# A decoder block on one Trainium2 core: the sums of one kept weight pair are tied, on VectorE, behind the last copies of a block inverse

## The chip, the cores and the metric

The kernel runs on one core of a Trainium2 chip. The metric is the device time of one execution in microseconds (us), less being better; a run's number is the median of its timed executions. The engines are called as in the profile: PE (TensorE, matrix products; PEld is its weight loads), DVE (VectorE), ACT (ScalarE), POOL (GpSimd) and SP (SyncE, which here only issues transfers). Each engine works through its own queue of instructions in order.

## The reference, cut to what matters

One transformer block on 256 tokens of width 2048, all in float32. A projection feeds two branches: a gated delta rule (heads of 128, solved in triangular blocks) and a sparse attention over the 64 best keys. Both are gated, merged, projected and normalised, and a gated feed-forward layer with a hidden width of 5632 follows.

```python
a = m + jnp.eye(CHUNK, dtype=f32)
u = lax.linalg.triangular_solve(a, v_beta, left_side=True, lower=True, unit_diagonal=True)
...
merged = jax.nn.sigmoid(gate_a) * (o_a @ w_branch_a[l]) + jax.nn.sigmoid(gate_b) * (o_b @ w_branch_b[l])
x = layer_norm(DEEPNORM_ALPHA * x + merged @ w_out[l], ln1_g[l], ln1_b[l])
h_gate, h_up = jnp.split(x @ w_ffn_in[l], 2, axis=-1)
x = layer_norm(DEEPNORM_ALPHA * x + (jax.nn.silu(h_gate) * h_up) @ w_ffn_out[l], ln2_g[l], ln2_b[l])
```

Two places of this computation meet in the change: the triangular solve (as an explicit inverse of each block) and the feed-forward weights of `w_ffn_in`.

## The kernel before, in words

**The stream of weights.** Nearly all of the time goes into products of the 256 tokens with weights that are streamed from memory. A weight chunk of 128 x 1024 goes through `chunk` (L84 to L94): SP issues its load into `raw` (L89), ACT rounds it to `hi` (L91), DVE takes the rest `lo = raw - hi` (L93), and PE multiplies with both parts. There are four buffers each of `raw`, `hi` and `lo`: SP's load waits until DVE has taken the `lo` of the chunk four places earlier, and ACT's cast waits until PE has finished that earlier chunk. In the stretch that the change touches, `group_ws` (L140) runs four chunks to a group; one chunk is sixteen matmuls of L153 and sixteen of L156, and a group's result is joined on ACT and DVE (L163, L164).

**Small work between the chunks.** After each chunk `tick` lets the waiting chains (generators) emit their next step, so that the work of the delta rule and of the attention stands between the chunks of the projection. Its products use four PSUM tiles called `aux`, the streams four called `acc`.

**Who sets the order.** PE's and SP's instructions stand as the code emits them. Those of DVE, ACT and POOL are put in order by a scheduler, from the data that they read and write and from a priority: `tc.high_priority(offset=LEAD)` moves a step forward, a negative offset moves it back.

**The block inverse.** `key_chain` inverts the triangular blocks: 32 x 32 blocks by substitution, then `merge(32)` and `merge(64)` (L589) join neighbouring blocks. A merge has three steps. L606 multiplies, two `aux` tiles, copied into `s_ak` by ACT (L612) and by DVE (L610). L617 transposes sixteen tiles in four groups of four, one `aux` tile a group; groups 0 and 2 are copied into `s_t` by ACT (L623), groups 1 and 3 by DVE (L621). L631 multiplies `s_t` with `s_ak`, and DVE puts the result into `s_u` (L638 in `merge(32)`, L636 in `merge(64)`). The `aux` tile of L617's last group is one that ACT's copy of group 0 (L623) sets free.

**The kept pairs.** The feed-forward products take pairs of weight rows with seven products in place of eight, for which sums of the weights are needed. For five groups (`KEPT`) the sums of the first pair are made early: `kept_chain` (L941) loads a pair into a raw buffer (L950, two transfers on SP), `four_sums` (L930) makes four sums on DVE (L934, L935, L938, L939), these are cast on ACT (L960) and their rests taken on DVE (L961), and POOL stores both (L963, L964) to memory (`d_s`), from where the feed-forward stage loads them from 851 us on. The chain takes pairs 0 to 3 one after another; pairs 0 and 2 use one raw buffer (`k_rawoh_`), pairs 1 and 3 another (`k_raws_x`), and all share one buffer for the casts (`k_hiol_`). So pair 2's load waits for pair 0's stores. All its DVE and ACT steps have a negative priority offset.

**What follows.** `late_form` writes `f_room` (L1059) into the buffer of pairs 1 and 3, so its first DVE instruction waits for the stores of pair 3; `z_chain` loads `z_wraw` into the buffer of pairs 0 and 2.

Of the kernel before, what the change touches and what calls it, by code (L numbers as in the profile page):

```python
# [8 lines left out]
F32 = mybir.dt.float32  # L9
# [3 lines left out]
OP = mybir.AluOpType  # L13
# [4 lines left out]
P = 128  # L18
# [14 lines left out]
LEAD = 70  # L33
# [30 lines left out]
def block_kernel(ctx: ExitStack, tc: tile.TileContext, xT, x, cpack, onehot, relb, convw, alog, dtb, gnw,  # L64
                 ws, wws, win, wz, wgt, wba, wbb, woa, wob, wfi, wfg, wfo, ln1g, ln1b, ln2g, ln2b, out):
    nc = tc.nc
# [3 lines left out]
    sm = ctx.enter_context(tc.tile_pool(name="sm", bufs=1, side="left"))  # L70
# [4 lines left out]
    def ps_aux():  # L75
        return aux.tile([P, 512], F32, name="aux", tag="aux")
# [42 lines left out]
    def event(name):  # L119
        done[name] = clock[0]  # L120
# [220 lines left out]
    def T(name, shape, dtype=F32, tag=None):  # L341
        return p1.tile(shape, dtype, name=name, tag=tag or name)
# [35 lines left out]
    def t16(name):  # L378
        return T(name, [P, NTB, H])
# [204 lines left out]

    rk2, rk, nb, nbe, rkb = t16("rk2"), t16("rk"), t16("nb"), t16("nbe"), t16("rkb")
    rq2, rq, fo = t16("rq2"), t16("rq"), t16("fo")
    d_m = dr.tile([4, NTB * H, 32, 32], F32, name="d_m")
    d_x = dr.tile([4, NTB * H, 32, 32], F32, name="d_x")

    def merge(b):  # L590

        n = P // (2 * b)
        hi = (64, P) if n == 1 else (0, P)
        w = 64 if n == 1 else 96
        uv = s_u.rearrange("p t (n two b) -> p t n two b", two=2, b=b)
        if n == 1:
            mp, up = mnv[:, :, 0:64], s_u[:, :, 0:64]
        else:
            mp = s_sq.rearrange("p (t c) -> p t c", c=64)
            up = s_e.rearrange("p a h d -> p (a h d)")[:, 0:1024].rearrange("p (t c) -> p t c", c=64)  # L600
            nc.scalar.copy(up.rearrange("p t (n b) -> p t n b", n=n), uv[:, :, :, 0, :])
        for q in range(2):
            a = ps_aux()
            for i in range(8):
                t = q * 8 + i
                nc.tensor.matmul(a[0:64, i * 64:(i + 1) * 64], mp[hi[0]:hi[1], t, :], uv[hi[0]:hi[1], t, :, 1, :],  # L606
                                 start=True, stop=True)
            dst = s_ak[0:64, q * 512:(q + 1) * 512]
            if q % 2:
                nc.vector.tensor_copy(dst, a[0:64])  # L610
            else:
                nc.scalar.copy(dst, a[0:64])  # L612
                yield 1
        for q in range(4):
            a = ps_aux()
            for i in range(4):
                nc.tensor.transpose(a[0:64, i * w:(i + 1) * w], up[0:w, q * 4 + i, :], ident[0:w, 0:w])  # L617
            dst = s_t[0:64, q * 4:q * 4 + 4, 0:w]
            src = a[0:64, 0:4 * w].rearrange("p (t d) -> p t d", t=4)
            if q % 2:  # L620
                nc.vector.tensor_copy(dst, src)  # L621
            else:
                nc.scalar.copy(dst, src)  # L623
            if q == 1:
                yield 1
        yield 2
        for q in range(2):
            a = ps_aux()
            for i in range(8):
                t = q * 8 + i  # L630
                nc.tensor.matmul(a[0:w, i * 64:(i + 1) * 64], s_t[0:64, t, 0:w], s_ak[0:64, t * 64:(t + 1) * 64],  # L631
                                 start=True, stop=True)
            dst = uv[0:w, q * 8:q * 8 + 8, :, 1, :]
            src = a[0:w].rearrange("p (t n b) -> p t n b", t=8, b=b)
            if n == 1:
                nc.vector.tensor_copy(dst, src)  # L636
            else:
                nc.vector.tensor_tensor(dst, src, dst, op=OP.add)  # L638
            yield 1 if q == 0 else 3


    def key_chain():
# [53 lines left out]
        yield INV_WAIT  # L696
        yield "qc1s"
        yield from merge(32)
        yield from merge(64)
        event("inv")  # L700

# [225 lines left out]

    d_s = dr.tile([len(KEPT), 2, P, 2, 1024], F32, name="d_s")

    def four_sums(ra, rb, lead=0):  # L930

        r0, r1, s0, s1 = (t[:, n * 512:n * 512 + 512] for t in (ra, rb) for n in range(2))
        with tc.high_priority(offset=lead):
            nc.vector.tensor_add(r0, r0, s1)  # L934
            nc.vector.tensor_add(s1, r1, s1)  # L935
        yield 1
        with tc.high_priority(offset=lead):
            nc.vector.tensor_add(r1, r0, r1)  # L938
            nc.vector.tensor_add(s0, r1, s0)  # L939

    def kept_chain(ms, wait, old, old_hi, gap, ev):  # L941
        yield wait
        raws = [T(f"k_raw{t}", [P, 2, 1024], tag=t) for t in old]
        hi = T(f"k_hi{old_hi}", [P, 2, 1024], F32R, tag=old_hi)
        for m in ms:
            if gap and m > ms[0]:
                yield gap
            raw = raws[m % len(old)]
            for i in range(2):
                nc.sync.dma_start(raw[:, i], wfg[KEPT[m] - 1, i])  # L950
                yield 1
            yield 1
            for _ in four_sums(raw[:, 0], raw[:, 1], -LEAD):
                yield 1
            yield 1
            for i in range(2):
                with tc.high_priority(offset=-LEAD):
                    for n in range(2):
                        cs = slice(n * 512, n * 512 + 512)
                        nc.scalar.copy(hi[:, i, cs], raw[:, i, cs])  # L960
                        nc.vector.tensor_sub(raw[:, i, cs].bitcast(F32R), raw[:, i, cs], hi[:, i, cs].bitcast(F32))  # L961
                yield 1
                nc.gpsimd.dma_start(d_s[m, 0, :, i], hi[:, i].bitcast(F32))  # L963
                nc.gpsimd.dma_start(d_s[m, 1, :, i], raw[:, i])  # L964
        event(ev)

    start(kept_chain(range(4), KEPT_FROM, ("oh_", "s_x"), "ol_", 0, "kept0"))
    conv_first(s_kT, pss)
    event("kc0")
# [193 lines left out]
    for tag in ("thi", "tlo"):  # L1163
        gates_home[tag][0] = 0
    start(early_chain(wgt[2], (2, 4), ga_ready, "gaready"))
    start(kept_chain(range(4, 5), 1, ("s_x",), "s_rv", 5, "kept1"))
    for j in range(4):
        js = slice(j * 512, (j + 1) * 512)
# [447 lines left out]
    for j in (1, 2, 3):  # L1616
        nc.vector.scalar_tensor_tensor(v1[j], v1[j], mv[:, 0:1], gt2[:, slice(j * 512, j * 512 + 512)],
                                       op0=OP.subtract, op1=OP.mult)
    for j in (1, 2, 3):
        nc.vector.scalar_tensor_tensor(v1[j], v1[j], rs, bt2[:, slice(j * 512, j * 512 + 512)],  # L1620
                                       op0=OP.mult, op1=OP.add)
# [113 lines left out]
```

## Time and profile before

| | us |
|---|---|
| median of 3 runs | 1452.83 |
| these runs | 1451.66, 1452.83, 1455.95 |
| the profiled execution's own time | 1453.58 |
| its span in the profile | 1451.8 |
| PE busy | 1443.1 |
| DVE busy | 1283.2 |
| ACT busy | 816.6 |
| POOL busy | 58.3 |

The span is what the hardware profiler saw from the first instruction to the last; the 1.8 us between it and the execution's own time lie around it. Starts in the timelines count from the start of the span. A row of a timeline gives start, duration, engine, line, operation, tile written and tile read, the count, and in brackets the idle time of the engine ahead of it and what ended that. The granted PE clock was 0.998 of full speed over the span.

### The profile page before, as it was taken

How to read it: one execution, taken by the hardware profiler on the slowest of the kernel's cores; microseconds unless marked ns; L12 is line 12 of the kernel's file. 1: busy time of each engine (PE TensorE's matmuls, PEld its weight loads, DVE VectorE, ACT ScalarE, POOL GpSimd, SP SyncE). 2: the span in 40 equal slices, each digit the busy share in tenths (PEclk: the TensorE clock that was granted, in tenths of full speed). 3: DMA queues.
4: the chain of work that ended last, by engine and by line, in shares of the span. 5: the costliest groups of instructions: out<-in, count | busy, mean ns of one | idle time of the engine just before them, and what ended most of it. 6: DMA issues, size and time to landing. Idle time of an engine off the chain costs nothing.

```text
span 1451.8 us, 19648 instructions
## 1 busy us (share of the span) xinstructions
PE 1443.1 (99%) x7137; PEld 1214.2 (84%) x7137; DVE 1283.2 (88%) x1769; ACT 816.6 (56%) x1025; POOL 58.3 (4%) x79
## 2 busy tenths in 40 slices
PE   9999999999999999999999999999999999999998
PEld 8888888888888888888888888888888888888886
DVE  6798988789799969998897899999999998989987
ACT  5765454557556646655445565656566565554552
POOL 0001011121000000000000000000000000000000
PEclk9999999999999999999999999999999999999999
DMA  8656589854456775766865777677766666888863
GB/s 290 196 162 196 174 213 335 287 188 159 171 202 221 264 248 201 249 186 208 296 210 202 244 263 281 244 267 257 279 214 211 213 218 247 313 338 269 318 210 116
DMA packets 102833, 339.81 MB, mean 234 GB/s; under 512 B 17792, under 2 KB 18984, under 8 KB 102224
## 3 DMA queue, kind: packets, MB, share of 16 engines
q1 hardware_dynamic: 88800, 311.35, 62.1%
q0 software_dynamic: 6752, 24.85, 5.0%
q10 hardware_dynamic: 7184, 2.36, 0.7%
q8 instruction: 56, 0.92, 0.3%
q14 instruction: 41, 0.34, 0.1%
HBM read 314.19 MB, written 24.31 MB: 233 GB/s over the span
## 4 chain that ended last, share of the span: by engine, by line
PE 98%; DMA 1%; ACT 0%; DVE 0%; issue 0%; POOLq 0%; SPq 0%; ACTq 0%; DVEq 0%
PE acc L217 11%; PE acc L218 11%; PE acc L219 11%; PE acc L153 10%; PE aux L217 10%; PE aux L219 10%; PE aux L218 10%; PE acc L156 5%; PE acc L173 4%; PE acc L175 4%; PE acc L174 4%; PE aux L174 2%; PE aux L175 2%; PE aux L173 1%; PE aux L737 1%; DMA k_rawoh__2366<-in_wfg_dram 1%
## 5 line engine op out<-in xcount | busy, mean ns | idle before, releaser
L91 ACT CAST hi<-raw 128x1024 fp32r<-128x1024 f32 (+1 forms) x384 | 392.9, 1033 | 326.7 <-PE acc L219 71.7
L93 DVE TENSOR_TENSOR lo<-raw,hi 128x1024 fp32r<-128x1024 f32 (+1 forms) x384 | 458.9, 1205 | 82.4 <-ACT hi L91 78.4
L153 PE MATMUL acc<-X,hi 128*128 128x512 f32 x640 | 203.7, 400 | 0.0
L217 PE MATMUL acc<-hi,X 128*128 128x512 f32 x370 | 145.2, 392 | 0.0
L219 PE MATMUL acc<-hi,X 128*128 128x512 f32 x370 | 144.1, 389 | 0.0
L218 PE MATMUL acc<-lo,X 128*128 128x512 f32 x370 | 144.0, 389 | 0.0
L156 PEld LDWEIGHTS acc<-X,lo 128*128 128x128 f32 x640 | 120.2, 188 | 28.3
L156 PE MATMUL acc<-X,lo 128*128 128x256 f32 x640 | 126.0, 278 | 0.0
L217 PE MATMUL aux<-hi,X 128*128 128x512 f32 x306 | 119.7, 391 | 0.0
L219 PE MATMUL aux<-hi,X 128*128 128x512 f32 x306 | 119.2, 389 | 0.0
L218 PE MATMUL aux<-lo,X 128*128 128x512 f32 x306 | 119.1, 389 | 0.0
L153 PEld LDWEIGHTS acc<-X,hi 128*128 128x128 f32 x640 | 97.5, 189 | 2.0 <-ACT hi L91 0.7
L241 ACT CAST f_thi<-f_wt 128x1024 fp32r<-128x1024 f32 x60 | 63.2, 1053 | 59.7 <-DVE f_wt L246 23.8
L219 PEld LDWEIGHTS acc<-hi,X 128*128 128x128 f32 x370 | 69.4, 188 | 14.5
L217 PEld LDWEIGHTS acc<-hi,X 128*128 128x128 f32 x370 | 69.5, 188 | 14.3 <-ACT s_u L979 0.4
L218 PEld LDWEIGHTS acc<-lo,X 128*128 128x128 f32 x370 | 69.5, 188 | 14.0
L242 DVE TENSOR_TENSOR f_tlo<-f_wt,f_thi 128x1024 fp32r<-128x1024 f32 x60 | 73.1, 1219 | 7.2 <-ACT f_thi L241 7.0
L219 PEld LDWEIGHTS aux<-hi,X 128*128 128x128 f32 x306 | 57.4, 188 | 12.0
L218 PEld LDWEIGHTS aux<-lo,X 128*128 128x128 f32 x306 | 57.5, 188 | 11.9
L217 PEld LDWEIGHTS aux<-hi,X 128*128 128x128 f32 x306 | 57.4, 188 | 11.7
L173 PE MATMUL acc<-hi,X 128*128 128x512 f32 x160 | 64.3, 402 | 0.0
L241 ACT CAST thi<-wt 128x1024 fp32r<-128x1024 f32 x36 | 37.9, 1053 | 46.2 <-DVE wt L246 29.6
(661 smaller groups left out, 3145.1 us busy)
## 6 DMA issues: line engine op xcount, KB each, us to landing
raw<-in_wfg_dram SPq DMA_DIRECT2D x125, 512.0 KB, 5.1
raw<-in_wws_dram SPq DMA_DIRECT2D x80, 512.0 KB, 4.2
raw<-in_wfo_dram SPq DMA_DIRECT2D x70, 512.0 KB, 5.1
raw<-in_wgt_dram SPq DMA_DIRECT2D x49, 512.0 KB, 3.7
f_wraw<-in_wfg_dram SPq DMA_DIRECT2D x30, 512.0 KB, 6.5
raw<-in_win_dram SPq DMA_DIRECT2D x21, 512.0 KB, 4.1
kept<-d_s SPq DMA_DIRECT2D x20, 512.0 KB, 7.7
wraw<-in_wfo_dram SPq DMA_DIRECT2D x18, 512.0 KB, 5.2
```

The source lines that it names most:

```text
L91: nc.scalar.copy(hi, raw)
L93: nc.vector.tensor_sub(lo, raw, hi.bitcast(F32))
L153: nc.tensor.matmul(pss[c], hv[:, kk, cs[c]], X2[k // 4][:, k % 4], start=(k == 0), stop=False, skip_group_check=True)
L156: nc.tensor.matmul(pss[c][:, :S], lv[:, kk, cs[c]], xh[:, k, :], start=False, stop=(k == KT - 1), skip_group_check=True)
L173: nc.tensor.matmul(ps, xh, hv[:, kk], start=(k == 0), stop=False)
L174: nc.tensor.matmul(ps, xh, lv[:, kk], start=False, stop=False)
L175: nc.tensor.matmul(ps, xl, hv[:, kk], start=False, stop=(k == 2 * n - 1))
L217: nc.tensor.matmul(o, sh, hi, start=first, stop=False)
L218: nc.tensor.matmul(o, sh, lo, start=False, stop=False)
L219: nc.tensor.matmul(o, sl, hi, start=False, stop=last)
L241: nc.scalar.copy(hi, v)
L242: nc.vector.tensor_sub(lo, v, hi.bitcast(F32))
```

## The change

A column `one` of 128 x 1, filled with 1.0 at the kernel's start, is added. DVE's copies of transposed groups in a merge (L621) become a multiplication by this column, read as an operand. For the third kept pair alone (index 2), the first of the four sums also reads the column, after a `memset` that fills it with 1.0 again. The numbers stay what they were. The `memset` writes what the copies read, so it must stand behind the last of them on DVE, and the sum that reads it stands behind the `memset`.

```diff
+    one = sm.tile([P, 1], F32, name="one")
+    nc.vector.memset(one, 1.0)
...
             if q % 2:
-                nc.vector.tensor_copy(dst, src)
+                nc.vector.tensor_scalar(dst, src, one[0:64], None, op0=OP.mult)
...
-    def four_sums(ra, rb, lead=0):
+    def four_sums(ra, rb, lead, pin):
...
-            nc.vector.tensor_add(r0, r0, s1)
+            if pin is None:
+                nc.vector.tensor_add(r0, r0, s1)
+            else:
+                nc.vector.memset(pin, 1.0)
+                nc.vector.scalar_tensor_tensor(r0, r0, pin, s1, op0=OP.mult, op1=OP.add)
...
-            for _ in four_sums(raw[:, 0], raw[:, 1], -LEAD):
+            for _ in four_sums(raw[:, 0], raw[:, 1], -LEAD, one if m == 2 else None):
```

The order on PE and SP stays as it was. On DVE, around the sums of pair 2 (`k_rawoh_`), this stood before; L610 and L621 are the copies of `merge(64)`:

```order
L93 TENSOR_TENSOR lo<-raw,hi 128x1024 x2
L934 TENSOR_TENSOR k_rawoh__2366<-k_rawoh__2366 128x512
L935 TENSOR_TENSOR k_rawoh__2366<-k_rawoh__2366 128x512
L938 TENSOR_TENSOR k_rawoh__2366<-k_rawoh__2366 128x512
L961 TENSOR_TENSOR k_rawoh__2366<-k_rawoh__2366,k_hiol__2368 128x512
L939 TENSOR_TENSOR k_rawoh__2366<-k_rawoh__2366 128x512
L610 COPY s_ak<-aux 64x512
L621 COPY s_t<-aux 64x4x64
L93 TENSOR_TENSOR lo<-raw,hi 128x1024
L961 TENSOR_TENSOR k_rawoh__2366<-k_rawoh__2366,k_hiol__2368 128x512 x2
L621 COPY s_t<-aux 64x4x64
L93 TENSOR_TENSOR lo<-raw,hi 128x1024
```

And this stands on DVE at the same place now; the new kernel's lines count two more from L588 on and six more behind the sums, so that L612 and L623 are the copies, L939 the `memset`, L940 to L945 the sums and L967 the rests:

```order
L93 TENSOR_TENSOR lo<-raw,hi 128x1024 x3
L612 COPY s_ak<-aux 64x512
L623 TENSOR_SCALAR s_t<-aux,one 64x4x64 x2
L93 TENSOR_TENSOR lo<-raw,hi 128x1024
L939 MEMSET one 128x1
L940 SCALAR_TENSOR_TENSOR k_rawoh__2368<-k_rawoh__2368,one 128x512
L941 TENSOR_TENSOR k_rawoh__2368<-k_rawoh__2368 128x512
L944 TENSOR_TENSOR k_rawoh__2368<-k_rawoh__2368 128x512
L945 TENSOR_TENSOR k_rawoh__2368<-k_rawoh__2368 128x512
L93 TENSOR_TENSOR lo<-raw,hi 128x1024
L967 TENSOR_TENSOR k_rawoh__2368<-k_rawoh__2368,k_hiol__2370 128x512
```

The copies and two `lo` have moved ahead of the sums. On ACT, the casts of pair 2's sums (L960) stood between the two halves of the inverse's copies (L612, then L623) before:

```order
L612 COPY s_ak<-aux 64x512
L960 CAST k_hiol__2368<-k_rawoh__2366 128x512 x2
L91 CAST hi<-raw 128x1024
L960 CAST k_hiol__2368<-k_rawoh__2366 128x512
L623 COPY s_t<-aux 64x4x64
L960 CAST k_hiol__2368<-k_rawoh__2366 128x512
L91 CAST hi<-raw 128x1024
L623 COPY s_t<-aux 64x4x64
```

Now they stand behind both of these copies (L614 and L625 in the new count, with L966 the casts):

```order
L614 COPY s_ak<-aux 64x512
L91 CAST hi<-raw 128x1024
L625 COPY s_t<-aux 64x4x64
L91 CAST hi<-raw 128x1024
L625 COPY s_t<-aux 64x4x64
L163 COPY s_pc<-acc 128x256 x2
L966 CAST k_hiol__2370<-k_rawoh__2368 128x512
L91 CAST hi<-raw 128x1024
L966 CAST k_hiol__2370<-k_rawoh__2368 128x512 x3
```

The four casts have moved behind the copies of groups 0 and 2, and so have POOL's stores that wait for them; for pair 3 POOL now has both stores of casts ahead of both stores of rests, where it had them in turn.

## The prediction, made blind

> **What bounds the kernel now.** I read the page first, then who waited for whom on PE, then the stretch around the change engine by engine. The first two lines of the page are its span and its busy times:
>
> ```profile
> span 1451.8 us, 19648 instructions
> PE 1443.1 (99%) x7137; PEld 1214.2 (84%) x7137; DVE 1283.2 (88%) x1769; ACT 816.6 (56%) x1025; POOL 58.3 (4%) x79
> ```
>
> PE is busy all but 1451.8 - 1443.1 = 8.7 us. The other engines matter only where they make PE wait. These are all of PE's waits (total, times, longest):
>
> ```profile
> PE acc L136 <- ACT hi L91: 1.7, 1, 1.7
> PE aux L421 <- DVE warm L417: 1.1, 1, 1.1
> PE aux L617 <- ACT s_t L623: 0.8, 1, 0.8
> PE aux L1612 <- ACT ct L1606: 0.7, 1, 0.7
> ```
>
> The first two lie at the kernel's start (its first products, L136, and the warm-up, L421), the fourth at its end. Together they are 4.3 us; the other 4.4 lie behind PE's last product, where the chain that ended last leaves PE:
>
> ```profile
> 1447.65 0.59 ACT x L1623
> ```
>
> The third is the only wait in between, and it stands in the block inverse that the change touches. PE there (start, duration):
>
> ```profile
> 251.73 0.63 PE L617 MATMUL aux<-ident,s_u 64*64 64x64 f32 x8
> 252.29 0.73 PE L153 MATMUL acc<-X,hi 128*128 128x512 f32 x2
> 253.10 0.62 PE L153 MATMUL acc<-X,hi 128*128 128x512 f32 x2
> ...
> 255.28 0.41 PE L617 MATMUL aux<-ident,s_u 64*64 64x64 f32 x4
> 256.51 0.41 PE L617 MATMUL aux<-ident,s_u 64*64 64x64 f32 x4 [0.81 <-ACT s_t L623]
> 256.85 0.73 PE L153 MATMUL acc<-X,hi 128*128 128x512 f32 x2
> 257.65 0.63 PE L153 MATMUL acc<-X,hi 128*128 128x512 f32 x2
> ```
>
> The last group of four transposes waited for an `aux` tile that ACT's copy of group 0 frees. Why ACT was late is read from ACT, then from DVE:
>
> ```profile
> 247.77 0.58 ACT L612 COPY s_ak<-aux 64x512 f32<-64x512 f32 x1 [0.21 <-PE aux L606]
> 253.37 1.35 ACT L960 CAST k_hiol__2368<-k_rawoh__2366 128x512 fp32r<-128x512 f32 x2 [5.02 <-DVE k_rawoh__2366 L934]
> 254.62 1.04 ACT L91 CAST hi<-raw 128x1024 fp32r<-128x1024 f32 x1
> ...
> 256.09 0.36 ACT L623 COPY s_t<-aux 64x256 f32<-64x256 f32 x1
> ```
>
> ```profile
> 247.59 1.23 DVE L93 TENSOR_TENSOR lo<-raw,hi 128x1024 fp32r<-128x1024 f32 x1 [1.34 <-ACT hi L91]
> 252.60 0.69 DVE L934 TENSOR_TENSOR k_rawoh__2366<-k_rawoh__2366 128x512 f32<-128x512 f32 x1 [3.78 <-DMA k_rawoh__2366<-in_wfg_dram]
> ```
>
> Pair 2's first sum stood at the head of DVE's queue for 3.78 us until its weights landed; the casts of the sums stood ahead of L623 in ACT's queue and waited 5.02 us with it. So the chain is: a late transfer, a sum, its casts, the inverse's copy, PE. Its price is what PE lost, not the 3.78 or 5.02 us.
>
> **The change part by part.** *The wait that goes.* By the idle row PE lost 0.81 us. By starts: from 255.28 to 256.85 eight transposes and the wait took 1.57 us; the undisturbed eight at 251.73 took 0.56 us until the next product at 252.29. The difference is 1.01 us, and starts are what the rest of the queue moves by, so I take 1.0.
>
> *What is late next.* On ACT only a cast of a weight chunk (L91) now stands ahead of L623. It needs its chunk and PE's release of the buffer. The chunk was asked for on SP at 243.28; its row, with the landing time last, and SP's:
>
> ```profile
> 243.28 0.33 SPq L89 DMA_DIRECT2D raw<-in_wws_dram  x1
> raw<-in_wws_dram SPq DMA_DIRECT2D x1, 512.0 KB, 6.7
> 250.34 0.39 PE L156 MATMUL acc<-X,lo 128*128 128x256 f32 x2
> ```
>
> It landed at 250.0, PE ended the older chunk at 250.73, so the cast (1.04 us) ends at about 251.8, the first group's transposes are there at 251.73 + 0.28 = 252.0, and the copy (0.36) ends at 252.4. PE wants the tile at 255.28 + 0.28 = 255.56: 3.1 us to spare. PE's order is unchanged, so nothing else comes between.
>
> *The wait that is added.* The `memset` and the pinned sum wait on DVE for the second copy L621, which waits for the last transposes at 255.56 to 255.84. Behind them on DVE are pair 2's other sums and the `lo` of a later chunk; on ACT the casts of the sums; on POOL the four stores of pair 2 (SP's loads of pair 3 wait for the stores of pair 1, so not for these). One `lo` stands between the copies and the `memset`; its cast waits for PE to end the chunk before the transposes, 255.3, so it runs 256.4 to 257.6 and the sums start at 257.7 instead of 252.60. That puts 5 us of delay on pair 2, and takes two `lo` and three copies out from behind a transfer. Pair 2's stores are not read until much later (loads on SP, first and last start):
>
> ```profile
> L1404 SPq DMA_DIRECT2D kept<-d_s x20: 326/503/1049, 850.9 to 1039.3; - x20
> ```
>
> So for PE the added wait is no cost.
>
> *The operations.* Rows for what is replaced, and the nearest ones for what replaces it (mean ns last):
>
> ```profile
> L621 DVE COPY s_t<-aux 64x384 f32<-64x384 f32 x2 | 1.1, 537 | 0.0
> L621 DVE COPY s_t<-aux 64x256 f32<-64x256 f32 x2 | 0.8, 407 | 0.0
> L813 DVE TENSOR_SCALAR sc<-rel,smt 128x256 f32<-128x256 f32 x1 | 0.3, 350 | 0.0
> L825 DVE TENSOR_SCALAR wk<-wk 128x256 f32<-128x256 f32 x1 | 0.3, 276 | 0.0
> L1284 DVE SCALAR_TENSOR_TENSOR x<-x,mv,lng 128x512 f32<-128x512 f32 x8 | 5.9, 744 | 0.0
> 1.03 0.06 DVE L417 MEMSET warm<- 128x1 f32 x1
> 3.46 0.29 DVE L445 CAST X<-s_vT 128x256 fp32r<-128x256 f32 x1 [2.37 <-DMA s_vT<-in_xT_dram]
> 227.67 0.54 DVE L621 COPY s_t<-aux 64x384 f32<-64x384 f32 x1
> 232.10 1.50 PE aux L631 x16
> ```
>
> No row has a multiplication by a column out of PSUM. Reading a column costs at most 350 - 276 = 74 ns on 128 x 256 (L813 reads one, L825 a constant), and the copy could at best become 407 - 350 = 57 ns shorter, so a copy changes by -0.06 to +0.07 us; I take 0, as the PSUM source stays. The pinned sum costs 744 ns in place of the 0.69 us at 252.60, 0.05 us more, each `memset` 0.06 us. Together under 0.5 us of DVE. All of it is covered: the first `memset` by the 2.37 us in which DVE waits for the tokens, `merge(32)`'s copies by the 3.9 us between the end of the last at 228.2 and its reader at 232.10, the rest by the 3.78 us of idle time that the new order fills. Without that cover it would cost PE at most its 0.5 us.
>
> [...]
>
> *The sum.* 1453.58 (the profiled execution's own time) - 1.0 = 1452.6; its span 1451.8 becomes 1450.8. That execution is 0.75 above the median of the runs, so from the median: 1452.83 - 1.0 = 1451.8. About 0.3%, 4.4 us, is what a measurement of this kernel can tell from no change; the forecast is a quarter of that.
>
> **The rivals.** *The wait comes back elsewhere.* ACT's copy could wait as long behind the chunk's cast if that chunk landed late. Pair 2's own load took the longest here:
>
> ```profile
> 243.66 8.85 DMA k_rawoh__2366<-in_wfg_dram
> ```
>
> With 8.85 in place of 6.7 us the chunk lands at 252.1 and the copy ends at 253.5, still 2 us early; against it too, the `lo` of two chunks come earlier, and so do SP's loads that wait for them. If it happened the gain would be nothing: 1452.8. That the change doesn't do what it says would give the same time; the order speaks against it, since sums and casts stand behind the copies on both engines. 0.13 together.
>
> *Slower: pair 2's late stores crowd pair 3.* The stores of rests (the first of two is shown) were issued here, and this is what came after (the windows row gives PE, PEld, DVE, ACT and POOL busy, the clock, the DMA share and GB/s):
>
> ```profile
> 259.60 0.53 POOL L964 DMA_DIRECT2D d_s<-k_rawoh__2366  x1 [1.80 <-DVE k_rawoh__2366 L961]
> 264.00:272.00 8.00, 8.00 (x56) 6.93 (x55) 3.68 (x5) 2.42 (x4) 0.00 (x0) 1.00 1.01 376
> 275.21 0.69 DVE L934 TENSOR_TENSOR k_raws_x<-k_raws_x 128x512 f32<-128x512 f32 x1 [1.61 <-DMA k_raws_x<-in_wfg_dram]
> 292.18 0.69 DVE L1059 TENSOR_TENSOR f_room<-X 128x512 f32<-128x512 f32 x1 [4.40 <-issue]
> 293.84 2.35 DVE L93 TENSOR_TENSOR lo<-raw,hi 128x1024 fp32r<-128x1024 f32 x2
> 303.99 0.40 PE L174 MATMUL acc<-lo,X 128*128 128x512 f32 x1
> ```
>
> Counting on from 257.7 (four sums of 0.7, a `lo`, the rests between joins) these two stores fall at about 266 and 267, into a stretch where the transfers already fill the engines. Their 1.05 MB at 376 GB/s is 2.8 us that pair 3's loads could land later. DVE would stand that much longer at pair 3's sum (275.21), pair 3's stores would go later, and `f_room` at 292.18, which waits for them, with the `lo` behind it. The first of these `lo` ends at 295.0 and PE wants it at 303.99, so 9.0 us (8.0 with PE 1.0 earlier) are free against 2.8. PE loses what goes beyond 8.0. To be told from no change it takes 1452.83 + 4.4 = 1457.2, a loss of 5.4 over the forecast and so a delay of 13.4 us. 0.05.
>
> *Faster by much more.* PE's busy time could hide slow products near the stall that go with it. Starts speak against that: pairs of products behind the transposes start 0.81 us apart at 252.29 to 253.10 and 0.80 at 256.85 to 257.65, ahead of the wait as behind it. Even all four listed waits are 4.3 us, so a gain of over 4.4 would need hidden time: 1452.83 - 4.4 = 1448.4. 0.02. [...]
>
> **How the numbers follow.** The forecast has 0.80, the three rivals 0.13, 0.05 and 0.02. The predicted time is the forecast's, 1451.8. The range holds the forecast and the first rival with the spread of runs that do not differ: the fastest run shown lies 1.2 us under the median, the slowest 3.1 above it. Below I go from 1451.8 down by 1.2 to 1450.6, above from the first rival's 1452.8 up by 1.2 to 1454.0, which leaves out the other two rivals and the odd run. Faster by over 0.3% gets 0.02, slower 0.05, and within 0.3% the forecast with the first rival, 0.93.
>
> **What would show it.** Right: in the list of PE's waits the one of L617 (L619 in the new count) on ACT is gone and the other three stand; the eight transposes take about 0.6 us with no gap in place of 1.57; DVE's wait for pair 2's load is gone, the first sum stands at about 257 and its wait is under 1 us; ACT's 5.02 us are gone; PE busy is near 1443, the span near 1450.8. Wrong: a wait of PE between 240 and 320 us on another line, the L619 row with a wait of 0.8 us on a cast, pair 3's sum waiting over 8 us for its load, or `f_room`'s wait at 12 us or more with a wait of PE near 304.

## The result and the profile after

The change made the kernel slower: 1466.27 us (median of 5 runs, 1465.84 to 1467.13) against 1453.37 for the kernel before on the same chip (5 runs, 1451.66 to 1455.95). The ratio is 1.0089, 95% interval 1.0078 to 1.0101, that is 12.9 us. The profiled execution took 1467.01 us, its span and busy times are:

```profile
span 1465.2 us, 19647 instructions
PE 1455.8 (99%) x7137; PEld 1213.3 (83%) x7137; DVE 1286.0 (88%) x1771; ACT 816.3 (56%) x1025; POOL 58.3 (4%) x79
```

The same 7137 matmul records, and PE is busy 12.7 us longer: 1455.8 for 1443.1. PE's waits (total, times, longest) are 5.2 us together for the 4.3 of before, so they are 0.9 us of the loss at most:

```profile
PE acc L136 <- ACT hi L91: 2.2, 1, 2.2
PE aux L421 <- DVE one L588: 1.1, 1, 1.1
PE acc L139 <- DVE lo L93: 1.0, 3, 0.5
PE aux L1618 <- ACT ct L1612: 0.7, 1, 0.7
PE acc L217 <- ACT s_u L985: 0.2, 1, 0.2
```

The wait of the block inverse is not among them. PE there (start, duration):

```profile
252.40 0.63 PE L619 MATMUL aux<-ident,s_u 64*64 64x64 f32 x8
...
255.95 0.64 PE L619 MATMUL aux<-ident,s_u 64*64 64x64 f32 x8
256.51 0.72 PE L153 MATMUL acc<-X,hi 128*128 128x512 f32 x2
```

The second eight take 0.56 us until the next product, as forecast. The first eight start 0.67 us later than before (251.73; in this execution PE waited more in the first 30 us, at L136 and L139), the product behind the second eight 0.34 us earlier (256.85). So here the change does what it says and gains 1.0 us. What the kernel loses, it loses later. A hundred us on, PE is still 0.10 us ahead; the first row below is of after, the second of before:

```profile
359.11 0.50 PE L217 MATMUL acc<-hi,X 128*128 128x512 f32 x1 [0.15 <-ACT s_u L985]
```

```profile
359.21 0.50 PE L217 MATMUL acc<-hi,X 128*128 128x512 f32 x1
```

The last copy to `x` starts at 1461.08 where it started at 1447.65, 13.4 us behind. Between, PE's lists have one wait, of 0.7 us near the end and in both (L1618, L1612 before), so the time went into the products themselves. Three groups of them, before and then after (count, busy us, mean ns of one):

```profile
L153 PE MATMUL acc<-X,hi 128*128 128x512 f32 x640 | 203.7, 400 | 0.0
L217 PE MATMUL aux<-hi,hH 128*128 128x512 f32 x114 | 44.5, 390 | 0.0
L217 PE MATMUL aux<-thi,hH 128*128 128x512 f32 x10 | 3.9, 390 | 0.0
```

```profile
L153 PE MATMUL acc<-X,hi 128*128 128x512 f32 x640 | 203.7, 400 | 0.0
L217 PE MATMUL aux<-hi,hH 128*128 128x512 f32 x114 | 45.2, 396 | 0.0
L217 PE MATMUL aux<-thi,hH 128*128 128x512 f32 x10 | 3.9, 389 | 0.0
```

In the last two rows line, shape and kind of weights are the same: with `hi` as the moving operand a product takes 6 ns more, with `thi` none. Starts show it without the modelled ends (before, then after):

```profile
1286.74 0.40 PE L217 MATMUL aux<-hi,hH 128*128 128x512 f32 x1
...
1288.79 0.39 PE L217 MATMUL aux<-hi,hH 128*128 128x512 f32 x1
```

```profile
1299.61 0.40 PE L217 MATMUL aux<-hi,hH 128*128 128x512 f32 x1
...
1301.01 0.40 PE L217 MATMUL aux<-hi,hH 128*128 128x512 f32 x1
```

Nine products in 2.05 us are 228 ns from start to start; six in 1.40 us are 233.

What tells `hi` from `thi` is where they lie. The pool `sm` gives the one-column tile 32 bytes in each partition, and the pools on the left side are stacked, so every tile allocated behind it moves by 32 bytes (`s_kT` from 58752 to 58784): `hH`, `hL`, `thi`, `tlo`, `gt`, `oh`, the forms. The chunks' `hi` and `lo` (from 25216) lie ahead of it, the input `X2` lies on the right side; these stay. `thi` and `hH` moved together, `hi` and `hH` apart.

### The profile page after: what moved, and what is told of

It reads as the page before. It is cut to its first block, busy times and chain, and to the rows that moved or that the text cites. A ratio compares the mean times of both kernels' runs of the same rounds, so it can differ in the third digit from the quotient of the medians.

```text
span 1465.2 us, 19647 instructions
## 1 busy us (share of the span) xinstructions
PE 1455.8 (99%) x7137; PEld 1213.3 (83%) x7137; DVE 1286.0 (88%) x1771; ACT 816.3 (56%) x1025; POOL 58.3 (4%) x79
## 4 chain that ended last, share of the span: by engine, by line
PE 73%; DVE 1%; DMA 1%; issue 0%; ACT 0%; POOLq 0%; DVEq 0%
PE acc L217 11%; PE acc L219 10%; PE acc L218 10%; PE aux L219 9%; PE aux L217 9%; PE aux L218 9%; PE acc L173 2%; PE acc L175 2%; PE acc L174 2%; PE aux L175 2%; PE aux L174 2%; PE aux L173 2%; DMA raw<-in_wfg_dram 1%; PE aux L1128 0%; PE aux L897 0%
## 5 line engine op out<-in xcount | busy, mean ns | idle before, releaser
L153 PE MATMUL acc<-X,hi 128*128 128x512 f32 x640 | 203.7, 400 | 0.0
L217 PE MATMUL acc<-hi,X 128*128 128x512 f32 x370 | 145.8, 394 | 0.2 <-ACT s_u L985 0.2
L218 PE MATMUL acc<-lo,X 128*128 128x512 f32 x370 | 144.4, 390 | 0.0
L217 PE MATMUL aux<-hi,X 128*128 128x512 f32 x306 | 120.2, 393 | 0.0
L218 PE MATMUL aux<-lo,X 128*128 128x512 f32 x306 | 119.5, 390 | 0.1
L153 PEld LDWEIGHTS acc<-X,hi 128*128 128x128 f32 x640 | 97.5, 189 | 2.0 <-ACT hi L91 0.7
L217 PEld LDWEIGHTS acc<-hi,X 128*128 128x128 f32 x370 | 69.5, 188 | 15.3 <-ACT s_u L985 0.6
L218 PEld LDWEIGHTS acc<-lo,X 128*128 128x128 f32 x370 | 69.5, 188 | 14.4
L218 PEld LDWEIGHTS aux<-lo,X 128*128 128x128 f32 x306 | 57.5, 188 | 12.5 <-DVE lo L93 0.5
L217 PEld LDWEIGHTS aux<-hi,X 128*128 128x128 f32 x306 | 57.5, 188 | 12.4
```

The source lines that it names most:

```text
L153: nc.tensor.matmul(pss[c], hv[:, kk, cs[c]], X2[k // 4][:, k % 4], start=(k == 0), stop=False, skip_group_check=True)
L217: nc.tensor.matmul(o, sh, hi, start=first, stop=False)
L218: nc.tensor.matmul(o, sh, lo, start=False, stop=False)
```

## The experiments

Each run of the kernel was timed in five rounds beside the kernel before. **Distance** below is the start of the weights that are loaded while a product runs (those of the next product) less the start of its moving operand, in bytes modulo 256; the starts of the tiles are those that the program gives them. That the next weights load meanwhile is in the traces: in before PE takes up the weights of an L218 from 1286.05 for 0.19 us while the L217 of 1286.04 is at work, and that L218 starts at 1286.27. Consecutive 512-column products are grouped by it, over all pairs that start under 260 ns apart (some 5000 of 5475; the others have other work or a wait between them):

| run | ratio to before, 95% interval | ns from start to start by distance (pairs) |
|---|---|---|
| before | | 0: 227.3 (5031) |
| after | 1.0089, 1.0078 to 1.0101 | 0: 228.4 (3384), 32: 233.1 (1328), 224: 233.3 (319) |
| pad64 | 1.0069, 1.0057 to 1.0082 | 0: 228.5 (3386), 64: 232.9 (1328), 192: 228.6 (319) |
| shift32 | 1.0084, 1.0070 to 1.0098 | 0: 228.5 (3385), 32: 233.1 (1328), 224: 233.3 (319) |
| left32 | 1.0117, 1.0102 to 1.0133 | 0: 227.2 (2042), 32: 232.9 (289), 224: 233.4 (2702) |
| all32 | 1.0028, 1.0018 to 1.0038 | 0: 227.0 (2042), 64: 226.5 (289), 192: 229.0 (2700) |
| pad192 | 1.0048, 1.0035 to 1.0061 | 0: 228.5 (3384), 64: 232.4 (319), 192: 229.2 (1328) |
| pad256 | 1.0005, 0.9996 to 1.0014 | 0: 227.3 (5026) |

The first theory was that starts that differ modulo 64 cost; its rivals were the new operations themselves, and any start off a multiple of 64.

**shift32: the layout alone.** The kernel before, with a column that nothing reads:

```diff
-    rq2, rq, fo = t16("rq2"), t16("rq"), t16("fo")
+    rq2, rq, fo = t16("rq2"), t16("rq"), t16("fo"); one = sm.tile([P, 1], F32, name="one"); nc.vector.memset(one, 1.0)
```

> The kernel before with the column allocated at the same place and set to one, and read by nothing: all the operations and their order are those of before. Theory 'unequal starts': the same 1689 products are slow and the wait of 0.8 us at L617 is there, 1467.3 us (before plus 13.9). Rival 'the operations themselves': 1453.4.

Measured: 1466.67 us, before 1454.15. The wait is there and the loss is there:

```profile
PE aux L617 <- ACT s_t L623: 1.0, 1, 1.0
```

The copies, the pinned sum and the order have no part in the loss that these times could show.

**pad64: the change with the column 64 bytes wide.**

```diff
-    one = sm.tile([P, 1], F32, name="one")
+    one = sm.tile([P, 16], F32, name="one")[:, 0:1]
```

> The change as it is, but the column's tile is 64 bytes wide in each partition where it was 32 as allocated, so that all tiles behind it keep their start modulo 64. Theory 'unequal starts' (a 512-column product is some 6 ns longer where its moving operand and the weights that are loaded meanwhile start at different bytes modulo 64; 1689 of 5476 products do so after the change, none before): the products go back to 226 to 228 ns from start to start, no wait of L617 or L619 on PE, 1452.4 us, that is the before kernel's time minus 1.0. Rival 'the operations themselves' (the pinned sums, the memset and the multiplying copies, or the order that they bring, slow the products): 1466, as after.

Measured: 1464.93 us. The theory said 1452.4, so its modulus is wrong. The group keeps its price:

```profile
L217 PE MATMUL aux<-hi,hH 128*128 128x512 f32 x114 | 45.0, 395 | 0.0
```

**left32: the chunks' pieces move too.** The kernel before with a column ahead of them:

```diff
-    ident = cst.tile([P, P], F32, name="ident")
+    ident = cst.tile([P, P], F32, name="ident"); off = cst.tile([P, 1], F32, name="off"); nc.vector.memset(off, 0.0)
```

> The kernel before with an unread column ahead of the chunks of weights, so that everything allocated on the left side behind the constants moves by 32 bytes (the pieces hi and lo too), and nothing on the right side (the input X2) does. Theory 'unequal starts': hi with hH and lo with hH are fast again, hi with X2 is slow: 3393 of 5476 products of 512 columns are unequal, by 6 ns 20 us, 1473 to 1476 us; the products of 1220 to 1440 us at 227 ns and those of 30 to 340 us longer than before. Rival 'any start off a multiple of 64 is slow': all 5476 are, by 6 ns 33 us, 1486 us. Rival 'the operations themselves': 1453.4.

Measured: 1472.22 us, just under the theory's 1473 to 1476. The slow and the fast groups have changed places:

```profile
L217 PE MATMUL acc<-hi,X 128*128 128x512 f32 x370 | 147.3, 398 | 0.0
L217 PE MATMUL aux<-hi,hH 128*128 128x512 f32 x114 | 44.4, 390 | 0.0
```

`hi` and `hH` both start 32 bytes further on and are as fast as before (390), `hi` with the unmoved `X` takes 398 for the 392 of before. So what costs here is the distance of two operands; the rival of the absolute start, with 1486, falls.

**all32: the right side moves too.** A second column beside the padding there, which moves `X2` the other way, since that side is filled downwards:

```diff
-    pad = padp.tile([P, 24], F32, name="pad")
+    offr = padp.tile([P, 1], F32, name="offr"); nc.vector.memset(offr, 0.0); pad = padp.tile([P, 24], F32, name="pad")
```

> As the run before, with a second unread column on the right side, so that every large tile starts at 32 modulo 64 and none is unequal. Theory 'unequal starts': 1453.4 us, as before, all products at 227 ns. Rival 'any start off a multiple of 64 is slow': 1486 us. Rival 'the operations themselves': 1453.4.

Measured: 1458.85 us, 4.7 above before, not the 1453.4 of the theory. The distance of `hi` and `X2` is here 64 or 192, not 0, and it matters: 229.0 ns at 192 for 227.0 at 0. With pad64, the modulus 64 fell twice.

**pad256 and sweep: what the modulus is.** The change with a tile of 256 bytes, and a kernel of products alone, one section of 48 products to a line, for example

```diff
+    one = sm.tile([P, 64], F32, name="one")[:, 0:1]
```

```
    p = ps(); [nc.tensor.matmul(p[i % 2], wt(i, 32), mv(0), start=i < 2, stop=i >= 46) for i in range(48)]; end(p)
```

> The change as it is with a column's tile of 256 bytes in each partition, so that the tiles behind it move by 256. The first theory (starts modulo 64) fell with the runs pad64 and all32. Its successor 'distance modulo 256': what counts is the distance between the start of the moving operand and the start of the weights that are loaded meanwhile; in the traces so far a distance of 0 modulo 256 takes 227 ns from start to start, 32 and 224 take 233, 64 takes 233 and 192 takes 229 in most stages. Then this run has the products of the kernel before and only the change's own effect: before minus 1.0 us, 1453 where before is 1454. Rival 'any move of the tiles costs' (by the share of SBUF that DMA or another engine uses at the same time): 1465. Rival 'the operations themselves': 1466.

> Not the kernel: it leaves out the whole computation and only multiplies a moving tile m of 512 columns by weights w on TensorE, 48 products to a section, each section a line of its own, with the other engines nearly idle. Lines 96 to 112: m at 0, w at 0, 4, 8, 16, 24, 32, 48, 64, 96, 128, 160, 192, 224, 256, 288, 320, 512 bytes behind it modulo 256. Lines 113 to 121 and 122 to 130: m moved by 32 and by 64, w from 0 to 256 in steps of 32. Lines 131 to 139: two products of 512 and two of 256 columns in turn, w from 0 to 256 in steps of 32. Lines 140 to 143: two pairs in turn, so that the distance to the own weights and to the weights loaded meanwhile differ. Theory 'distance modulo 256': 227 ns from start to start at 0, 256 and 512, 233 at 32, 64 and 224, 229 at 192, the same where m and w move together; lines 140 and 142 (own weights at the same start, the next product's at another) slow, 141 and 143 fast. Rival 'another engine or a DMA makes the products slow': all sections alike, at 227. Rival 'the absolute start decides': lines 113 to 130 slow where m or w lies off a multiple of 256, at 32 and 32 too.

Measured: pad256 took 1454.27 us, before 1453.61; the products are back at 227.3 ns and the loss of after is gone. The groups of the sweep (distance 32, 128, 192, 256 on lines 101, 105, 107, 109; m and w moved together by 32 on line 114):

```profile
L101 PE MATMUL acc<-m,w 128*128 128x512 f32 x48 | 11.3, 395 | 0.0
L105 PE MATMUL acc<-m,w 128*128 128x512 f32 x48 | 11.3, 395 | 0.0
L107 PE MATMUL acc<-m,w 128*128 128x512 f32 x48 | 11.2, 392 | 0.0
L114 PE MATMUL acc<-m,w 128*128 128x512 f32 x48 | 11.1, 390 | 0.0
L109 PE MATMUL acc<-m,w 128*128 128x512 f32 x48 | 11.1, 389 | 0.0
```

Line 96, the first section, is left out, since its products are slow at the kernel's start (a mean of 434 ns where the other sections' 512-column products have 389 to 397). By starts, the first five of a section left out: 226.7 at 256, 226.9 at 512, 227.0 and 226.7 where both moved by 32 and by 64; 228.9 at 192; 230.7 at 8, 231.0 at 24, 232.4 at 4 and at 128; 233.3 to 234.2 at 16, 32, 48, 64, 96, 160, 224, 288 and 320. In these sections the distance modulo 256 decides, with no transfer under way (a DMA share of 0.00 from 50 to 500 us) and no other engine at work but VectorE, which copies out the end of each section, so the rival of another engine or a transfer falls. The alternating lines 140 to 143 gave 231.6, 230.2, 231.8 and 231.6: all slow, which the theory had not said.

**sweep2: which distance.** Sections in which only the own weights, or only the next ones, lie at another distance.

> Not the kernel: as the run sweep, products of a moving tile m by weights w on TensorE alone, 48 to a section and a section to a line. What is to be told apart is which distance costs: that of the moving operand to its own weights, or that to the weights that are loaded meanwhile (the next product's). Lines 97 and 98: distance 0 (227 ns) and 32 (233). Line 103: m and w both at 0, 0, 0, 32 in turn, so that the own distance is always 0 and the next weights differ in two of four. Line 104: m at 0, 0, 0, 32 and w at 32, 0, 0, 0, so that the next weights are always at distance 0 and the own differ in two of four. Theory 'weights loaded meanwhile': 104 at 227, 103 at 230. Rival 'own weights': 103 at 227, 104 at 230. Rival 'any change of start from product to product': both at 229 or more, as lines 99 (w at 0 and 32 in turn), 100 (m at 0 and 32 in turn), 101 and 102 (every fourth). Lines 107 to 122: two products of 512 and two of 256 columns in turn, as in L153 and L156, the weights of the 512s at 0, 64, 192, 224 and within each those of the 256s at 0, 64, 192, 224; lines 131 to 138 of the run sweep gave 175.4 ns for a product of the four at 0 and 0 and 173.8 at 192 and 192, so 107 at 175.4 and 117 at 173.8.

Measured:

```profile
L98 PE MATMUL acc<-m,w 128*128 128x512 f32 x48 | 11.4, 396 | 0.0
L103 PE MATMUL acc<-m,w 128*128 128x512 f32 x48 | 11.3, 394 | 0.0
L104 PE MATMUL acc<-m,w 128*128 128x512 f32 x48 | 11.3, 394 | 0.0
L100 PE MATMUL acc<-m,w 128*128 128x512 f32 x48 | 11.2, 392 | 0.0
L97 PE MATMUL acc<-m,w 128*128 128x512 f32 x48 | 11.1, 389 | 0.0
```

By starts line 103 has 231.5 and line 104 230.9 ns; the rival of any change of start holds, and the two distances stay untold apart. One product in four out of step slows its neighbours too: line 101, with the weights of every fourth product moved by 32, has 231.7 ns, where one product of 233.4 to three of 226.7 would give 228.4. The kernel shows the same: in after, a pair at distance 0 takes 226.7 ns where the twelve products ahead of it were all 512 columns wide and at 0 (1335 pairs), and 229.5 where three or more of them were not at 0 (1249 pairs). This is why distance 0 has 228.4 in the table for after.

**pad192: the sweep's prices in the kernel.** As pad256, with `[P, 48]`.

> The change with a column's tile of 192 bytes in each partition. Theory 'distance modulo 256', with the prices of the run sweep: 1364 products of 512 columns get the distance 192 (228.9 ns against 226.7, 3.0 us), 325 the distance 64 (233.4, 2.2 us), and those beside them 1 to 3 us as in after and pad64: before plus 5 to 8 us, 1459 to 1462 where before is 1454, well below the 1465 of pad64, in which the two distances change places. Rival 'any distance but 0 costs alike': 1465.

Measured: 1461.65 us, before 1453.63. The medians are 8.0 us apart, the ratio gives 7.0 (5.1 to 8.9), where 5 to 8 were expected.

**early: where the gained microsecond goes.** In pad256 the products are those of before, the wait at the inverse is gone, and still nothing is gained. PE's longest wait there is a new one; the row, and the copy it waits for:

```profile
357.96 0.50 PE L217 MATMUL acc<-hi,X 128*128 128x512 f32 x1 [1.20 <-ACT s_u L985]
```

```profile
357.32 0.59 ACT L985 COPY s_u<-acc 128x512 f32<-128x512 f32 x1
```

In before the same copy (L979) ended at 358.57 + 0.59 = 359.16 and PE's product started at 359.21, without a wait in the list: no slack. The copy stands on ScalarE behind a conversion (L208) that waits for VectorE's L314 (1.03 us in before, 2.19 here). By the timelines PE is 2.53 us earlier here than in before (its transposes of `s_e` start at 350.02 for 352.55; 1.5 us of that is a quicker start of the kernel, 1.0 the change), L314 only 1.25 us (355.05 for 356.30); the rest of PE's lead ends as a wait. The edit to pad256 puts the copy two instructions forward:

```diff
-            nc.scalar.copy(dst[:, tb, j * 512:(j + 1) * 512], ps)
+            with tc.high_priority(offset=30): nc.scalar.copy(dst[:, tb, j * 512:(j + 1) * 512], ps)
```

> The run pad256 with one more edit: the second copy of a block's product out of PSUM to s_u (L985, ScalarE) stands two instructions earlier in its engine's order, ahead of one hi piece and one s_in copy (0.95 and 0.48 us). In the profile of pad256 the wait of 1.0 us at L617 was gone and PE waited 1.2 us at 359 us for this copy, with the copy's end at 357.91. Theory 'given back behind the next late copy': with the copy 1.4 us earlier PE's wait at L217 is below 0.2 us and products from 360 us on start 1.0 to 1.2 us earlier against the before kernel's than in pad256; in time 1.0 to 2.2 us less than before, 1451.5 to 1452.7 where before is 1453.6. Rival 'VectorE's and the loads' pace at 330 to 360 us holds PE': the wait moves to another line within 10 us, and the time is that of pad256.

Measured: 1453.19 us, before 1454.10, ratio 0.9995 (0.9986 to 1.0005). The product and the copy:

```profile
358.10 0.50 PE L217 MATMUL acc<-hi,X 128*128 128x512 f32 x1 [0.16 <-ACT s_u L985]
```

```profile
357.46 0.58 ACT L985 COPY s_u<-acc 128x512 f32<-128x512 f32 x1
```

The copy ends at 358.04. Behind the `hi` piece and the `s_in` copy (0.95 and 0.48 us) it would have ended at 359.47, and PE's 0.16 us would have been 1.6. Of PE's start against before, 0.97 us are gained at the inverse and 0.23 given back here.

The rest is given back later. At 820 us PE waits for a `lo` of VectorE's in early, and not in before; PE's products there, in before and then in early:

```profile
819.73 0.39 PE L217 MATMUL aux<-hi,X 128*128 128x512 f32 x1
819.96 0.40 PE L218 MATMUL aux<-lo,X 128*128 128x512 f32 x1
820.20 0.39 PE L219 MATMUL aux<-hi,X 128*128 128x512 f32 x1
```

```profile
818.60 0.39 PE L217 MATMUL aux<-hi,X 128*128 128x512 f32 x1
819.49 0.50 PE L218 MATMUL aux<-lo,X 128*128 128x512 f32 x1 [0.49 <-DVE lo L93]
819.82 0.40 PE L219 MATMUL aux<-hi,X 128*128 128x512 f32 x1
```

From the first to the third are 0.47 us in before and 1.22 in early, so 0.75 us are lost. VectorE's work ahead of this `lo` begins with a sum that waits for a load (L246, in before and then in early):

```profile
814.84 1.22 DVE L246 TENSOR_TENSOR f_wt<-f_wraw,raw 128x1024 f32<-128x1024 f32 x1 [2.45 <-DMA raw<-in_wfg_dram]
```

```profile
814.49 1.22 DVE L246 TENSOR_TENSOR f_wt<-f_wraw,raw 128x1024 f32<-128x1024 f32 x1 [3.25 <-DMA raw<-in_wfg_dram]
```

SP asked for this load (L282) at 809.55 in before and at 808.39 in early, 1.16 us sooner, but the sum starts only 0.35 us sooner; why, the runs don't show. With 0.97 gained, 0.23 and 0.75 given back, nothing is left of the change's gain in this execution. It is the same in pad256: of the 2.5 us by which PE is ahead of before at 350 us, 1.3 are lost at 359 us, 0.3 at 582 and 1.0 at 820, from where on PE is 0.1 behind before. In time the interval holds both no change and the forecast of 1.0 less, so the time itself doesn't tell them apart.

**early_alone: the same edit to the kernel before.**

> The kernel before with the one edit by which the run early differs from pad256, the copy to s_u two instructions earlier on ScalarE (L979 here). Theory 'given back behind the next late copy': in before PE came to this copy's release with nothing to spare and without a wait, so the edit alone brings 0.0 to 0.3 us; the wait of 0.8 to 1.2 us at L617 is there. Rival 'the copy's place is worth the microsecond by itself': before minus 1.0.

Measured: 1453.94 us, before 1453.63, ratio 0.9999 (0.9989 to 1.0008); the wait at L617 is there with 1.6 us, more than expected. (Behind this wait, from 256.5 to 260.0 us, the granted clock was 0.58 in this execution, where before has 1.00, and 512-column products of L153 started 427 ns apart, so its starts are not set against those of before.) The copy's place is worth nothing by itself, and with the change it only moves the loss from 359 to 820 us. No run is faster than before by more than its interval; pad256 and early are both faster than after.

## Why the prediction was wrong

**The wait that goes: right.** 1.0 us forecast; 1.57 us became 0.56.

**What is late next: right for this tile, and looked for in too short a stretch.** ACT's copy had 3.1 us to spare by the forecast. In after it stands here:

```profile
252.85 0.37 ACT L625 COPY s_t<-aux 64x256 f32<-64x256 f32 x1 [0.55 <-PE aux L619]
259.07 0.62 ACT L966 CAST k_hiol__2370<-k_rawoh__2368 128x512 fp32r<-128x512 f32 x1 [1.40 <-DVE k_rawoh__2368 L940]
```

PE wants the tile 0.28 us into the transposes at 255.95, at 256.23, so 3.0 us were free. But the prediction looked for new waits from 240 to 320 us only. The next hand-over without slack lay at 359 us and another at 820 us, and pad256 shows that the forecast would have failed even with the layout unhurt: its interval, 0.9996 to 1.0014, leaves out the 0.9993 of 1.0 us less. The rival "the wait comes back elsewhere", given 0.13 with an earlier place for it, is what that run does.

**The added wait: right.** Sums at 257.7, stores at about 266 and 267, pair 3's sum and `f_room` with waits as before. After has, from VectorE and then from POOL:

```profile
258.18 0.06 DVE L939 MEMSET one<- 128x1 f32 x1
258.29 0.75 DVE L940 SCALAR_TENSOR_TENSOR k_rawoh__2368<-k_rawoh__2368,one 128x512 f32<-128x512 f32 x1
...
277.17 0.69 DVE L937 TENSOR_TENSOR k_raws_x<-k_raws_x 128x512 f32<-128x512 f32 x1 [1.74 <-DMA k_raws_x<-in_wfg_dram]
...
292.99 0.69 DVE L1065 TENSOR_TENSOR f_room<-X 128x512 f32<-128x512 f32 x1 [4.27 <-DMA d_s<-k_raws_x]
```

```profile
266.32 0.53 POOL L970 DMA_DIRECT2D d_s<-k_rawoh__2368  x1 [3.29 <-DVE k_rawoh__2368 L967]
```

258.29 less the 0.67 us of the late start is 257.6; POOL issues the second store of rests at 267.52. The rival of the crowded loads, with 13.4 us of delay needed, did not come: the two waits are 1.74 and 4.27 for 1.61 and 4.40.

**The operations: their bounds held, the value taken was too low.** A multiplying copy out of PSUM was bounded at -0.06 to +0.07 us and taken at 0:

```profile
L623 DVE TENSOR_SCALAR s_t<-aux,one 64x256 f32<-64x256 f32 x2 | 0.9, 472 | 2.1 <-PE aux L619 2.1
```

It is 472 ns for the copy's 407, so +0.065 and near the upper end. The 65 ns are about what reading a column cost on SBUF in before (350 - 276 = 74); the source stayed in PSUM, so the reason given for 0 did not hold. The work was covered, as the forecast said.

**The step that failed** is the sum, 1453.58 - 1.0, which lets all other products keep their time. The change part by part costed the column's `memset` and its readers, and not the tile: its 32 bytes were put at nothing without a reason. PE's order is unchanged, as the prediction says, but the same order doesn't mean the same pace. Put with the table's means, what PE lost is 1328 x 5.8 ns = 7.7 us at distance 32, 319 x 6.0 ns = 1.9 us at 224, and 3384 x 1.1 ns = 3.7 us at distance 0 beside them: 13.3 us. With the 0.67 us of the start, the 1.0 gained and 0.15 waited at 359 us this makes 13.1 of the 13.4 us between the two spans.

**The rival "faster by much more"** asked whether PE's busy time hides slow products, and answered it from starts around the wait alone. That was the right question with the other sign, and L153, where it looked, is a group that the move left as it was (400 and 400 ns). PE's busy share does not tell the two kernels apart: it is 99% in both profiles, 13.4 us of span apart.

## What to carry to other kernels

A small tile is not free because its operations are: in stacked pools it moves everything allocated behind it (in shift32 by 32 bytes, at a ratio of 1.0084), and the layout of the products' operands belongs in the costing of a change, compared before and after. Where operands start at equal places modulo 256 a new tile is rounded up to 256 bytes, as pad256 did (227.3 ns, as in before); putting it behind all others should do as well, but was not tried. And a gain on the bounding engine is followed downstream to every hand-over that has no slack, however far off (here 100 and 560 us), since another engine or a load that is not sped up can take it back there: PE waited 1.20 us for ScalarE's copy at 359 us in pad256, and lost 0.75 at 820 us in early, behind VectorE's `lo`.

## What the runs showed of the hardware

- In the sweep a 512-column product (fp32r operands, 128 x 128 weights) follows the last of its kind in 226.7 to 227.0 ns when moving operand and weights start at equal places modulo 256 bytes, and in 229 to 234 ns when not; a shift of 4 bytes is enough (232.4). Moving both by 32 or by 64 costs nothing (227.0 and 226.7). Why the period is 256, and whether it is the loading of the weights that takes the time, the runs don't show.
- Where two products of 512 and two of 256 columns take turns 0 was not the best of the distances tried. In the sweep the mean of the four is 175.4 ns at 0 and 173.8 at 192; in sweep2 it was 175.6 and 173.8 where all four were at 0 or at 192, and 174.6 to 179.2 in the fourteen other mixtures. In L153 the pairs take 233.2 ns in before (distance 0) and 226.5 in all32 (64), and between 37 and 250 us, where most of this stage runs, PE gains 0.6 us on before in all32. What a kernel with such a distance in this stage alone would gain was not tried.
